# Feed-forward of a two-layer decoder trunk: another placing of the second product's slab jobs, 22 pairs instead of 24 in its right half, later gathers, and four PSUM banks for the last transposes

## The chip, the cores and the metric

The kernel runs on one core of a Trainium2 chip. The metric is the device time of one execution in microseconds, the median over several runs; lower is better. A profile comes from one execution of its own.

## The reference, cut to what matters

Two decoder layers on 256 tokens of width 2048, all in float32. Each layer ends with a squared-ReLU feed-forward of inner width 8192, and that is the part that the change touches:

```python
def squared_relu_mlp(h, w1, w2):
    z = jax.nn.relu(h @ w1)
    return (z * z) @ w2
...
for i in range(DEPTH):                      # DEPTH = 2
    ...                                     # pooling mixer or differential attention
    x = x + jnp.concatenate([token_out, mem_out], axis=-1) @ w_out[i]
    x = x + squared_relu_mlp(rms_norm(x, ffn_norm[i]), w_ff1[i], w_ff2[i])
```

w_ff1 is 2048x8192 and w_ff2 8192x2048, 64 MB each and layer; they are read from DRAM once and used once.

## The kernel before

**Numbers as two halves.** Each float32 operand is split in two: a rounded high part (ACT, a cast, L170) and the remainder (DVE, a subtraction, L173). A product is then high times high, high times low and low times high. For the weights this split runs all through the kernel: SP loads rows of 128x1024 (L139) into four "raw" buffers, ACT and DVE split them into a ring of six slots of 512 columns (hi_ring, lo_ring, and two more called slot), TensorE reads the slots. `Feed` does this in a fixed order: `fill` (L209) prepares up to three jobs ahead of the one that is used, and `load` (L125) issues loads three rows ahead of that.

**Up tiles.** `ffn` (L820) computes the transposed hidden layer in 64 up tiles, "f" 0 to 63. A tile is 16 blocks of 128x128 weights: `narrow` (L906) issues for each block one matmul of the high part with 512 columns (L913) and one of the low part with 256 columns (L915), all into one PSUM bank, x_bank, that `bank` (L973) draws. While slab jobs hold seven banks, one bank of the tag st is left for it. ACT copies the bank out (L927), and after each second tile `convert` (L861) makes of the two tiles a pair: add, ReLU, square, high and low parts into a "spot" of za or zb, and four sums of quarters with their own high and low parts into another spot. There are 16 spots; `left` gives one back when the last reader of its pair is done.

**Slab jobs.** The second product runs while the up tiles still do, by a Strassen scheme with seven products for eight. `slab_jobs` (L976) treats one pair (two blocks of 128 rows of w_ff2) and one half of the output columns, A (the right 1024, called with c + 2) or B (the left 1024), as four jobs, 0 to 3, with 2, 1, 2 and 2 products of three 512-column matmuls each (L1004 to L1006). They accumulate over the pairs of a phase in seven banks, m0 to m2, n0, n1, o and t (`open_banks`, L1013).

The weights of a slab come as two rows. Row a is loaded by SP (L139), and half of row b is then added into it by an accumulating DMA of POOL (L141); row b is loaded by SP. Both use the three buffers of the tag rows: row a of slab n takes the buffer that row b of slab n-2 leaves when the low part of that slab's job 3 has been split off; job 0 needs row a with its sum, job 2 and job 3 need row b after the DVE addition at L204.

**Phases and bank changes.** The banks hold one half of the columns at a time, so PHASES (L285) takes the pairs in five stretches: A 0 to 5, B 0 to 11, A 6 to 17, B 12 to 23, A 18 to 31. Between two of them comes a bank change, `finish_banks` (L1020): ACT copies two banks (L1037, L1038), seven DVE additions (L1039 to L1045) combine the seven products into four corners, and later ticks run the rest, a tick being four blocks of an up tile: `gather` (L1052) adds what an earlier phase of the same half left in DRAM (accumulating POOL DMAs, L1054), `park` (L1056) stores the corners to DRAM (SP, L1058) when the half is not complete, and `scale` (L1067) and `turn` (L1075) scale a complete half, transpose it on TensorE (L1082) and add it to the residual (DVE, L1085).

**What sets the order.** `ffn_plan` (L289) writes the sequence of tiles and jobs. In the gap ahead of each tile it places up to RATE = 4 jobs of the running phase, if the pair is ready; behind the last job of a phase it places the change and no job until the next gap. A pair becomes ready every second tile, so in phase 0 every second gap has four jobs and the others none. From then on a period is one up tile and one slab. B columns of pairs 24 to 31 are left to eight down tiles "d" (`down_tile`, L937), each 16 blocks like an up tile.

Of the kernel before, what the change touches and what calls it, by code (L numbers as in the profile page):

```python
# [18 lines left out]
P = 128  # L19
# [263 lines left out]
STEPS = (1, 2, 3, 4, 6, 7, 8, 10)  # L283
NB = 24
PHASES = (("A", 0, 6), ("B", 0, 12), ("A", 6, 18), ("B", 12, 24), ("A", 18, 32))  # L285
RATE = 4


def ffn_plan(tiles):  # L289

    ready = {}
    for t, what in enumerate(tiles):
        if what[0] == "f" and what[1] % 2:
            ready[what[1] // 2] = t + LAG
# [3 lines left out]
    credit = 0  # L303
    phase = 0
    for t, what in enumerate(tiles):
        credit = min(credit + RATE, 4)
        first = len(items)
        while jobs and credit and ready[jobs[0][1]] <= t and jobs[0][0] == phase:
            items.append(("s", *jobs.pop(0)))
            credit -= 1  # L310
# [39 lines left out]
def program(ctx, tc, plan, dry, xT, memT, par, lam, cst, wst, yT):  # L350
# [469 lines left out]
    def ffn(l, xs, tag, done):  # L820
# [18 lines left out]
        def take():  # L839
            return spare.pop(0)  # L840

# [19 lines left out]
        def convert(i, late):  # L861
# [16 lines left out]
            def high():  # L878
                zat[i] = take()
                due[i] = ["A"] + (["B"] if i < NB else ["N"] * 8)  # L880
                nc.scalar.copy(zs(i)[:, :, 0:T], u)
# [12 lines left out]
            def sums_high():  # L894
                sat[i] = take()
                nc.scalar.copy(sit(i)[:, 0:512].rearrange("p (a c) -> p a c", a=2), sums)
# [40 lines left out]
        def down_tile(q, n, ps):  # L937
            ks = list(range(q * NK, q * NK + NK))
            if l == 1 and q == 3 and n == 7:
                narrow(ps, "w_ff2", n, ks[:12], z)  # L940
# [3 lines left out]
                for k in ks[12:]:  # L944
                    hi, lo = feed.block(("w_ff2", l, k, n, 1))
                    zk = z(k)
                    nc.tensor.matmul(end[:, 0:T], hi, zk[:, 0:T], start=k == ks[12], stop=False)
# [4 lines left out]
                for i in range(24, 32):  # L952
# [7 lines left out]
            for i in range(24, 32):  # L960
# [59 lines left out]
        def finish_banks(p):  # L1020
# [87 lines left out]
        def go(part):  # L1108
            for at_, what in part:
                if what[0] == "s":  # L1110
# [32 lines left out]

        return last, first_down - ups + 4 * 8

# [601 lines left out]
```

## Time and profile before

| what | value |
|---|---|
| device time, median of 3 runs | 2066.78 us (2066.61 to 2066.79) |
| the profiled execution's own time | 2067.66 us |
| its span in the trace | 2065.5 us, 30343 instructions |
| granted TensorE clock over the span | 0.996 |
| DMA | 435.61 MB, 211 GB/s over the span |

The profile is of one execution. Busy times of engines overlap; a busy TensorE is a modelled figure, since matmuls are pipelined. In the timeline a row gives the start in us from the start of the span, the duration, the engine, the line of the kernel, the operation with out<-in, and in square brackets how long the engine had been idle before it and what ended that wait. The feed-forward of the first layer lies at about 252 to 960 us, that of the second at about 1356 to 2060 us.

### The profile page before, as it was taken

Reading aid. Unit: us, or ns where it says so; the run is one execution under the profiler, and the core shown is the slowest. Engines: PE = TensorE matmul, PEld = TensorE weight load, DVE = VectorE, ACT = ScalarE, POOL = GpSimd, SP = SyncE. Lnnn points to the kernel's source line nnn. Section 1 sums busy time; section 2 is a strip of 40 time slices with the busy share of each in tenths; the row PEclk is TensorE's granted clock in tenths of the full one; section 3 lists DMA queues with packets and bytes.
Section 4 is the critical chain, followed back from the end, with each engine's and each line's share of the span. In section 5 each row is a group of like instructions: output and inputs, shape, how many; then the busy total and the mean of one; then the engine's idle time right before and its main releaser. Section 6 shows DMA issues by size and latency. Waiting matters only on the chain.

```text
span 2065.5 us, 30343 instructions
## 1 busy us (share of the span) xinstructions
PE 2016.9 (98%) x10592; PEld 1709.4 (83%) x10592; DVE 1764.8 (85%) x2641; ACT 1368.9 (66%) x2177; POOL 166.2 (8%) x195
## 2 busy tenths in 40 slices
PE   9999999999998999999999999999999999998998
PEld 7888888788886887887888899888878787887887
DVE  8988777999998998988775798877889898898987
ACT  7765566666676666667665697556667676676674
POOL 0002300000001010000000000410000001001000
PEclk9999999999999999999999999999999999999999
DMA  9565656777777786766655645656677778777775
GB/s 312 171 207 187 198 185 207 220 229 235 233 230 229 227 243 201 227 184 205 207 190 190 194 145 177 193 176 205 214 226 230 234 225 236 228 228 214 221 219 159
DMA packets 133642, 435.61 MB, mean 211 GB/s; under 512 B 15152, under 2 KB 18224, under 8 KB 133488
## 3 DMA queue, kind: packets, MB, share of 16 engines
q1 hardware_dynamic: 114912, 398.00, 58.2%
q0 software_dynamic: 18432, 35.66, 10.4%
q8 instruction: 83, 1.36, 0.3%
q14 instruction: 71, 0.58, 0.1%
q10 hardware_dynamic: 144, 0.01, 0.0%
HBM read 422.46 MB, written 8.39 MB: 209 GB/s over the span
## 4 chain that ended last, share of the span: by engine, by line
PE 88%; DMA 6%; DVE 4%; ACT 2%; issue 1%; POOL 0%; SPq 0%; ACTq 0%; POOLq 0%; DVEq 0%
PE x_bank L913 20%; PE x_bank L915 10%; PE p L1006 7%; PE p L1004 7%; PE p L1005 7%; PE wo L504 6%; DMA slab<-in_w 4%; PE wo L506 3%; PE q L535 3%; PE ff L913 3%; PE k L535 3%; PE v L535 3%; PE u L504 2%; PE mk L535 2%; PE mv L535 2%; DVE lo_ring L173 2%
## 5 line engine op out<-in xcount | busy, mean ns | idle before, releaser
L173 DVE TENSOR_TENSOR lo_ring<-raw,hi_ring 128x512 fp32r<-128x512 f32 (+1 forms) x643 | 553.2, 878 | 106.6 <-ACT hi_ring L170 99.2
L170 ACT CAST hi_ring<-raw 128x512 fp32r<-128x512 f32 (+1 forms) x643 | 483.0, 767 | 197.4 <-PE wo L504 61.6
L173 DVE TENSOR_TENSOR lo_ring<-slab,hi_ring 128x1024 fp32r<-128x1024 f32 x336 | 345.5, 1043 | 62.7 <-ACT hi_ring L170 58.1
L170 ACT CAST hi_ring<-slab 128x1024 fp32r<-128x1024 f32 x336 | 304.3, 906 | 115.4 <-DMA slab<-in_w 54.3
L141 POOL DMA_DIRECT2D slab<-in_w x112 | 96.8, 864 | 1648.4 <-ACT hi_ring L170 319.5
L913 PE MATMUL x_bank<-fx,hi_ring 128*128 128x512 f32 x704 | 221.5, 396 | 3.4 <-ACT room L927 3.4
L927 ACT COPY room<-x_bank 128x512 f32<-128x512 f32 x118 | 69.2, 586 | 208.9 <-PE x_bank L915 208.9
L170 ACT CAST slot<-slab 128x1024 fp32r<-128x1024 f32 x112 | 117.4, 1048 | 80.3 <-PE x_bank L913 80.1
L173 DVE TENSOR_TENSOR slot<-slab,slot 128x1024 fp32r<-128x1024 f32 x112 | 136.8, 1222 | 30.0 <-ACT slot L170 30.0
L504 PE MATMUL wo<-cat,hi_ring 128*128 128x512 f32 x512 | 161.6, 396 | 0.0
L915 PEld LDWEIGHTS x_bank<-fx,lo_ring 128*128 128x128 f32 x704 | 132.2, 188 | 31.1
L913 PE MATMUL x_bank<-fx0b,hi_ring 128*128 128x512 f32 x472 | 148.2, 395 | 0.0
L915 PE MATMUL x_bank<-fx,lo_ring 128*128 128x256 f32 x704 | 138.4, 278 | 0.0
L204 DVE TENSOR_TENSOR slab<-slab,slab 128x1024 f32<-128x1024 f32 x112 | 136.5, 1219 | 0.0
L1004 PE MATMUL p<-hi_ring,zb 128*128 128x512 f32 x280 | 112.3, 401 | 7.0 <-ACT hi_ring L170 7.0
L506 PEld LDWEIGHTS wo<-cat,lo_ring 128*128 128x128 f32 x512 | 96.1, 188 | 22.0
L913 PEld LDWEIGHTS x_bank<-fx,hi_ring 128*128 128x128 f32 x704 | 108.9, 189 | 6.4 <-ACT room L927 4.4
L1006 PE MATMUL p<-lo_ring,zb 128*128 128x512 f32 x280 | 109.6, 396 | 3.0 <-DVE lo_ring L173 2.8
L1005 PE MATMUL p<-hi_ring,zb 128*128 128x512 f32 x280 | 110.2, 393 | 0.0
L915 PEld LDWEIGHTS x_bank<-fx0b,lo_ring 128*128 128x128 f32 x472 | 88.7, 188 | 21.0
L506 PE MATMUL wo<-cat,lo_ring 128*128 128x256 f32 x512 | 101.7, 278 | 0.0
L915 PE MATMUL x_bank<-fx0b,lo_ring 128*128 128x256 f32 x472 | 92.7, 278 | 0.0
(525 smaller groups left out, 4679.3 us busy)
## 6 DMA issues: line engine op xcount, KB each, us to landing
raw<-in_w SPq DMA_DIRECT2D x500, 512.0 KB, 4.5
slab<-in_w SPq DMA_DIRECT2D x224, 512.0 KB, 3.5
slab<-in_w POOLq DMA_DIRECT2D x112, 256.0 KB, 4.7
part<-room SPq DMA_DIRECT2D x6, 512.0 KB, 4.4
room<-part POOLq DMA_DIRECT2D x4, 512.0 KB, 7.8
memraw<-in_mem SPq DMA_DIRECT2D x4, 512.0 KB, 3.6
memraw<-in_mem SPq DMA_DIRECT2D x6, 256.0 KB, 6.0
part<-c_x SPq DMA_DIRECT2D x6, 256.0 KB, 4.7
```

The costliest lines, as they stand in the source:

```text
L141: self.nc.gpsimd.dma_start(t[:, 512:1024], self.wst[other, :, 512:1024], accum_op=ALU.add)
L170: cast = self.nc.scalar.copy(hi, src)
L173: self.nc.vector.tensor_sub(lo, src, hi.bitcast(F32))
L204: add(two, t.unsqueeze(1).to_broadcast([P, 2, 512]), two)
L504: nc.tensor.matmul(ps, hi, xs[:, k, :], start=first and j == 0, stop=False)
L506: nc.tensor.matmul(ps[:, T : 2 * T], lo, xs[:, k, 0:T], start=False, stop=last and j == len(ks) - 1,)
L535: nc.tensor.matmul(ps[t], a, b, start=i == 0 and j == 0, stop=i == NK - 1 and j == 2)
L913: nc.tensor.matmul(ps, hi, src(k), start=k == ks[0], stop=False)
L915: nc.tensor.matmul(ps[:, T : 2 * T], lo, src(k)[:, 0:T], start=False, stop=k == ks[-1])
L1004: nc.tensor.matmul(ps, al, hi[:, s], start=i == begin, stop=False)
L1005: nc.tensor.matmul(ps, ah, hi[:, s], start=False, stop=False)
L1006: nc.tensor.matmul(ps, ah, lo[:, s], start=False, stop=i == end - 1)
```

## The change

- NB becomes 22: the B half is done by slab jobs for pairs 0 to 21 only, and the eight down tiles take pairs 22 to 31, 20 blocks each. Their rows are prepared in single jobs of 512 columns (rows_whole off), the up tiles' in whole rows as before.
- RATE and its credit go. A gap of phase 0 takes up to two jobs; the first gap behind a change two, the next three, then four; the last eight tiles two to four by what is left. Since the phases no longer begin with four jobs, job 0 of the next slab now stands in the gap of jobs 1 to 3 of the slab before, and the gap of a change lacks one job.
- The gather of the middle changes comes at tick 10 instead of 5, the park behind it at 15 instead of 9, the first park at 6 instead of 5, the scale of B at 15 instead of 9; the transposes of B begin one gap later and stand behind two jobs. The gather of the last phase stays at 5.
- The four transposes of the last A phase use banks t, o, n0 and n1, one each, instead of t four times.
- There are two more spots. They lie in the memory of the residual's second half (resid.parts[1], 1 MB), which is stored to DRAM at the start of ffn and reloaded behind job 3 of pair 29 in the last phase. `take` gives these two only to pairs and sums that are read out early.

```diff
-NB = 24
-PHASES = (("A", 0, 6), ("B", 0, 12), ("A", 6, 18), ("B", 12, 24), ("A", 18, 32))
-RATE = 4
+NB = 22
+PHASES = (("A", 0, 6), ("B", 0, 12), ("A", 6, 18), ("B", 12, 22), ("A", 18, 32))
...
-        credit = min(credit + RATE, 4)
+        room = 2 if phase == 0 else min(4, 2 + since)
+        if t >= len(tiles) - 8:
+            room = min(4, max(2, len(jobs) - 2 * (len(tiles) - 5 - t)))
+        since += 1
...
-                    turns = {t + 3 + h: h for h in range(4)}
+                    turns = {t + 4 + h: h for h in range(4)}
                 phase += 1
+                since = 0
                 break
...
-            items.insert(first + 1, ("turn", turns[t]))
+            items.insert(first + 2, ("turn", turns[t]))
...
+        kept = dp.tile([P, NK // 2, T], F32, tag="kept", name=f"kept{l}")
+        nc.sync.dma_start(kept, resid.parts[1])
+        more = sp.tile([P, 4, 512], F32R, tag="residb", name=f"more{l}")
+        spots += [more[:, 2 * j : 2 * j + 2, :] for j in range(2)]
...
-            ks = list(range(q * NK, q * NK + NK))
+            ks = list(range(2 * NB, 4 * NK))
...
-                at(5, gather)
+                at(5 if p == len(PHASES) - 1 else 10, gather)
...
-                at(5 if old is None else 9, park)
+                at(6 if old is None else 15, park)
...
-                t4 = bk("t" if half == "A" else "st", "ct", (P, 2, T))
+                t4 = bk(("t", "o", "n0", "n1")[h] if half == "A" else "st", "ct", (P, 2, T))
...
-                at(9, scale)
+                at(15, scale)
...
+                    if (p, i, j) == (4, 29, 3):
+                        assert {16, 17} <= set(spare)
+                        resid.parts[1] = sp.tile(
+                            [P, NK // 2, T], F32, tag="residb", name=f"resid_b{l}"
+                        )
+                        nc.sync.dma_start(resid.parts[1], kept)
...
+                    feed.rows_whole = False
                     down_tile(*what[1:], ps)
```

Three places show how rows move. The first is TensorE in phase 0 of the first layer; x_bank_2930 and x_bank_2978 are the banks of two successive up tiles. Before:

```order
L913 MATMUL x_bank_2930<-fx0b_1740,hi_ring_76 128x512 x2
L915 MATMUL x_bank_2930<-fx0b_1740,lo_ring_77 128x256 x2
L913 MATMUL x_bank_2978<-fx0a_1739,hi_ring_76 128x512 x2
L915 MATMUL x_bank_2978<-fx0a_1739,lo_ring_77 128x256 x2
L913 MATMUL x_bank_2978<-fx0a_1739,hi_ring_76 128x512 x2
```

The same border in the changed kernel, where x_bank_2915 and x_bank_2981 are the two tiles (line numbers are eight higher); p3 to p6 are products of a slab's jobs 2 and 3:

```order
L921 MATMUL x_bank_2915<-fx0b_1740,hi_ring_76 128x512 x2
L923 MATMUL x_bank_2915<-fx0b_1740,lo_ring_77 128x256 x2
L1012 MATMUL p3_2895<-slot0_2625,za0_2622 128x512
L1013 MATMUL p3_2895<-slot0_2625,za0_2622 128x512
L1014 MATMUL p3_2895<-slot0_2625,za0_2622 128x512
...
L1014 MATMUL p6_2898<-lo_ring_77,za0_2622 128x512
L921 MATMUL x_bank_2981<-fx0a_1739,hi_ring_76 128x512 x2
L923 MATMUL x_bank_2981<-fx0a_1739,lo_ring_77 128x256 x2
```

Two jobs, twelve matmuls, now stand between two tiles that were next to each other.

The second place is SP's queue at the third bank change of the first layer, with the corners' stores (part<-c_x, c_y, room), the slab rows (slab) and the up tiles' rows (raw). slab_5514 and slab_5591 are row b of slab 12 and row a of slab 13, slab_5597 and slab_5693 row b of 13 and row a of 14. Before:

```order
L139 DMA slab_5514<-in_w 128x1024
L139 DMA slab_5591<-in_w 128x1024
L139 DMA raw_5709<-in_w 128x1024
L139 DMA raw_5777<-in_w 128x1024
L1058 DMA part_5628<-c_x 128x512
L1058 DMA part_5628<-c_y 128x512
L139 DMA slab_5597<-in_w 128x1024
L139 DMA raw_5795<-in_w 128x1024
L1058 DMA part_5628<-room_2624 128x1024
L139 DMA slab_5693<-in_w 128x1024
```

After, where slab_5798 and slab_5840 are row b of slab 13 and row a of slab 14:

```order
L139 DMA slab_5661<-in_w 128x1024
L139 DMA slab_5750<-in_w 128x1024
L139 DMA raw_5828<-in_w 128x1024
L139 DMA raw_5838<-in_w 128x1024
L1066 DMA part_5772<-c_x 128x512
L1066 DMA part_5772<-c_y 128x512
L139 DMA raw_5903<-in_w 128x1024
L139 DMA raw_5922<-in_w 128x1024
L1066 DMA part_5772<-room_2624 128x1024
L139 DMA slab_5798<-in_w 128x1024
L139 DMA slab_5840<-in_w 128x1024
```

Row b of slab 13 moves behind the last store; the stores keep their place between row a of 13 and row a of 14.

The third place is DVE in a steady period. slab_5954 is row b of a slab, slab_6031 row a of the next, lo_ring<-slab a split. Before:

```order
L204 TENSOR_TENSOR slab_5954<-slab_5948,slab_5954 128x1024
L885 TENSOR_TENSOR zb_2623<-room_2624,zb_2623 128x2x256
L889 TENSOR_TENSOR room_2624<-room_2624 128x256
L892 TENSOR_TENSOR room_2624<-room_2624 128x128
L173 TENSOR_TENSOR lo_ring<-slab_5954,hi_ring 128x1024
L173 TENSOR_TENSOR slot_2625<-raw_6047,slot_2625 128x1024
L900 TENSOR_TENSOR zb_2623<-room_2624,zb_2623 128x512
L173 TENSOR_TENSOR lo_ring<-raw_6112,hi_ring 128x1024
L173 TENSOR_TENSOR lo_ring<-slab_6031,hi_ring 128x1024
L201 TENSOR_TENSOR slab_6031<-slab_6031 128x512
```

After, with slab_6065 and slab_6148 as rows b and slab_6096 as row a of the next slab:

```order
L204 TENSOR_TENSOR slab_6065<-slab_6010,slab_6065 128x1024
L173 TENSOR_TENSOR lo_ring<-slab_6065,hi_ring 128x1024
L173 TENSOR_TENSOR lo_ring<-slab_6096,hi_ring 128x1024
L878 TENSOR_TENSOR room_2624<-room_2624 128x2x256
L201 TENSOR_TENSOR slab_6096<-slab_6096 128x512
L173 TENSOR_TENSOR lo_ring<-raw_6158,hi_ring 128x1024
L173 TENSOR_TENSOR slot_2625<-raw_6177,slot_2625 128x1024
L173 TENSOR_TENSOR lo_ring<-slab_6096,hi_ring 128x512
L173 TENSOR_TENSOR lo_ring<-slab_6148,hi_ring 128x1024
L893 TENSOR_TENSOR za_2622<-room_2624,za_2622 128x2x256
L204 TENSOR_TENSOR slab_6148<-slab_6096,slab_6148 128x1024
```

The split of row a's job 0 now follows that of job 3 directly, and the two raw rows come between job 0 and job 3 of one slab instead of ahead of job 0.

More of the change, by code (lines that the diff above doesn't have):

```diff
@@ L302, in ffn_plan @@
     turns = {}
-    credit = 0
-    phase = 0
+    phase = since = 0
     for t, what in enumerate(tiles):
-        credit = min(credit + RATE, 4)
+        room = 2 if phase == 0 else min(4, 2 + since)
+        if t >= len(tiles) - 8:
+            room = min(4, max(2, len(jobs) - 2 * (len(tiles) - 5 - t)))
+        since += 1
         first = len(items)
-        while jobs and credit and ready[jobs[0][1]] <= t and jobs[0][0] == phase:
+        while jobs and room and ready[jobs[0][1]] <= t and jobs[0][0] == phase:
             items.append(("s", *jobs.pop(0)))
-            credit -= 1
+            room -= 1
             if not jobs or jobs[0][0] != phase:
@@ L878, in high @@
             def high():
-                zat[i] = take()
+                zat[i] = take(i >= NB)
                 due[i] = ["A"] + (["B"] if i < NB else ["N"] * 8)
@@ L894, in sums_high @@
             def sums_high():
-                sat[i] = take()
+                sat[i] = take(i > 28)
                 nc.scalar.copy(sit(i)[:, 0:512].rearrange("p (a c) -> p a c", a=2), sums)
@@ L937, in down_tile @@
         def down_tile(q, n, ps):
[L938 removed]
+            ks = list(range(2 * NB, 4 * NK))
             if l == 1 and q == 3 and n == 7:
[L940 removed]
+                narrow(ps, "w_ff2", n, ks[:-4], z)
                 end = mmt("end")
@@ L943, in down_tile @@
                 add_down(n, douts[downs[0] % 2])
-                for k in ks[12:]:
+                for k in ks[-4:]:
                     hi, lo = feed.block(("w_ff2", l, k, n, 1))
                     zk = z(k)
-                    nc.tensor.matmul(end[:, 0:T], hi, zk[:, 0:T], start=k == ks[12], stop=False)
+                    nc.tensor.matmul(end[:, 0:T], hi, zk[:, 0:T], start=k == ks[-4], stop=False)
                     nc.tensor.matmul(end[:, 0:T], hi, zk[:, T : 2 * T], start=False, stop=False)
@@ L951, in down_tile @@
                 tick()
-                for i in range(24, 32):
+                for i in range(NB, 32):
                     left(i, "N")
@@ L959, in down_tile @@
             narrow(ps, "w_ff2", n, ks, z)
-            for i in range(24, 32):
+            for i in range(NB, 32):
                 left(i, "N")
@@ L1142, in last @@
             feed.rows_whole = False
-        return last, first_down - ups + 4 * 8
+        return last, first_down - ups + 4 * (32 - NB)
     big = sp.tile([P, 4096], F32, tag="big", name="big0")
```

6 lines of the change are left out of this document (4 added, 2 removed).

## The prediction

> **What bounds the kernel now.** I read the page first, for the share of each engine, then the timeline of TensorE for the price of a tile and a slab, then the table of windows, to set each stretch of the feed-forward against its content, and last the waits and the chain of waits where a stretch came out too long.
>
> ```profile
> span 2065.5 us, 30343 instructions
> PE 2016.9 (98%) x10592; PEld 1709.4 (83%) x10592; DVE 1764.8 (85%) x2641; ACT 1368.9 (66%) x2177; POOL 166.2 (8%) x195
> 663.01 0.62 PE L913 MATMUL x_bank<-fx0a,hi_ring 128*128 128x512 f32 x2
> 668.59 0.40 PE L1004 MATMUL p<-slot,zb 128*128 128x512 f32 x1
> ```
>
> TensorE is the bound; DVE, at 85%, is next. An up tile runs from 663.01 to 668.59, 5.58 us, so a block of sixteen is 0.349. Columns of the windows: stretch, length, busy time and instructions of PE, PEld, DVE, ACT and POOL, granted clock, DMA share, GB/s.
>
> ```profile
> 290.79:375.05 84.26, 80.88 (x426) 68.71 (x425) 68.83 (x85) 53.87 (x72) 4.30 (x5) 1.00 0.66 206
> 375.05:419.19 44.14, 42.62 (x214) 34.72 (x213) 40.87 (x49) 29.34 (x37) 3.43 (x4) 1.00 0.77 234
> 419.19:501.96 82.77, 82.77 (x426) 70.44 (x424) 77.02 (x92) 57.46 (x73) 6.90 (x8) 1.00 0.78 231
> 501.96:545.99 44.03, 42.56 (x213) 34.79 (x212) 40.94 (x49) 29.37 (x37) 3.45 (x4) 1.00 0.77 238
> 628.76:678.70 49.94, 44.09 (x214) 34.41 (x212) 40.94 (x49) 28.92 (x37) 4.98 (x6) 1.00 0.80 231
> 761.47:831.92 70.45, 67.16 (x335) 55.10 (x334) 62.55 (x75) 46.16 (x59) 6.47 (x8) 0.98 0.73 216
> 893.92:959.65 65.73, 59.65 (x317) 50.99 (x316) 54.18 (x85) 43.90 (x71) 1.72 (x2) 0.95 0.56 173
> 1394.74:1479.01 84.27, 80.89 (x426) 68.72 (x425) 68.84 (x85) 53.88 (x72) 4.30 (x5) 1.00 0.67 203
> 1479.01:1524.32 45.31, 43.11 (x213) 34.62 (x212) 40.85 (x49) 29.32 (x37) 3.43 (x4) 1.00 0.76 231
> 1606.99:1653.12 46.13, 43.41 (x214) 34.55 (x212) 40.87 (x49) 29.34 (x37) 3.45 (x4) 1.00 0.73 223
> 1735.94:1784.85 48.91, 44.88 (x213) 35.75 (x212) 40.94 (x49) 28.93 (x37) 4.98 (x6) 0.97 0.83 237
> 1867.64:1939.12 71.48, 66.14 (x336) 53.66 (x335) 62.55 (x75) 46.31 (x59) 7.06 (x9) 1.00 0.76 215
> 2001.22:2059.80 58.58, 55.94 (x312) 48.06 (x311) 45.44 (x64) 31.07 (x41) 1.72 (x2) 1.00 0.57 174
> ```
>
> The third row is a steady stretch: eight periods of one up tile and one slab without a wait, 82.77 / 8 = 10.35 each, so a slab is 10.35 - 5.58 = 4.77 and one of its seven products 0.68. Every other row is set against that.
>
> - Phase 0 (rows 1 and 8): ten tiles and five slabs are 79.65; lost 4.61 and 4.62, together 9.2.
> - Bank changes: four periods are 41.38, so rows 2, 4 and 5 lose 2.76, 2.65 and 8.56, rows 9 to 11 lose 3.93, 4.75 and 7.53. Rows 6 and 12 hold six periods (62.08) and four transposes at 0.45 (1.8): 6.57 and 7.60. Together 44.35.
> - Tails (rows 7 and 13): eight down tiles (44.64), two slabs (9.54) and four transposes are 55.98; the second ends four blocks earlier, 54.59. Lost 9.75 and 3.99, together 13.74.
>
> In all 67.3 us of 2067.66 are no work, and the change turns on these.
>
> ```profile
> PE p L1004 <- ACT hi_ring L170: 12.0, 15, 2.5
> PE x_bank L913 <- ACT room L927: 8.1, 12, 0.7
> PE p L1006 <- DVE lo_ring L173: 6.3, 13, 0.6
> PE ct L1082 <- DVE residb L1085: 5.5, 2, 4.2
> 291.85 0.73 PE L913 MATMUL x_bank<-fx0a,hi_ring 128*128 128x512 f32 x2 [0.68 <-ACT room L927]
> 948.11 0.47 PE L1082 MATMUL ct<-const,c_a 128*128 128x128 f32 x1 [4.17 <-DVE residb L1085]
> 954.07 0.27 PE L1082 MATMUL ct<-const,c_b 128*128 128x128 f32 x1
> 954.28 0.27 PE L1082 MATMUL ct<-const,c_b 128*128 128x128 f32 x1
> ```
>
> The last two start 0.21 apart with one between them: about 0.11 per transpose, 0.45 for the four of a turn.
>
> **The change, part by part.**
>
> *Two jobs a gap in phase 0.* The waits on the eviction (L927) come where two up tiles share the one bank back to back; a lost 4.61 over five such borders is 0.92 each. Two jobs, 12 matmuls or about 2 us, now stand at every border, more than 0.92. Saved 9.2.
>
> *The ramp 2, 3, 4 and the missing job behind a change.* One up tile more stands ahead of the jobs that need the first copied bank, and DVE's seven additions and the splits queued behind them get 5.58 us more. Changes 0-1 and 1-2 lose 2.65 to 4.75 now; 5.58 more covers that, but the additions still sit ahead of the splits on a DVE that is 93% busy in steady gaps (77.02 of 82.77). I leave 1.0 each, ends 0 and 2.65.
>
> *The later gather, third change.*
>
> ```profile
> 622.69 0.68 DVE L1039 TENSOR_TENSOR c_y<-c_x,p 128x512 f32<-128x512 f32 x1
> 637.48 0.33 SPq L1058
> 637.90 7.98 DMA slab<-in_w
> 646.43 6.62 DMA slab<-in_w
> 653.20 1.06 ACT hi_ring L170
> 654.28 1.23 DVE lo_ring L173
> ```
>
> The additions begin at 622.69, the change's end. The store of the gathered corners (L1058) cannot go before the gather has landed, at end + 14.8, and row a of slab 14 is queued behind it on SP: it is loaded in 7.98, summed in 6.62 and ready at 653.05, end + 30.4. The changed order keeps that sequence. Job 0 of slab 14 is wanted after three tiles and fourteen products, 3 x 5.58 + 14 x 0.68 = end + 26.3; with cast and split ahead of it the stall is 4 to 6. The later tick moves the gather in the written order only: on POOL it follows the sum for slab 13 in both, so I let it land no later (if the tick, four blocks or 1.4 us, were a time, five of them would add 7). Jobs 2 and 3 of slab 13 need their row at end + 23.5 instead of 17.9. So 4.5 remains of 8.56 and 7.53, ends 1 and 11. At the fourth change, where nothing is parked, 1.5 remains of 6.57 and 7.60, ends 0 and 6.57. Per layer the changes keep 1 + 1 + 4.5 + 1.5 = 8, both layers 16.
>
> A wait of 4.5 us in one piece has a second price: behind the 4.17 us wait at 948.11 the transposes took 0.47 us where the later ones took 0.27. At half speed for at most the 5.9 us up to the rows at 954, that is up to 2.5 a layer. My sum leaves it out, since waits on splits were 2.5 us at the longest.
> The Trainium skill (TensorE: Matmul & The Clock Gate, section "Why this matters for your kernels") asks for no idle gaps of over some 3 us, since one window of idle halves the clock; the trace agrees with it at 948.11, and by it the time would be some 5 us above mine, 2038.
>
> *22 pairs instead of 24.* A layer gains 8 tiles x 4 blocks = 32 blocks x 0.349 = 11.16 and loses two slabs, 9.54: +1.6, both layers +3.2.
>
> *Turns of B* stand behind two jobs and share the bank st with x_bank; I put 1 a layer, ends 0 and 2: 2.
>
> *Steady periods.* A slab's chain runs through two periods, 20.70.
>
> ```profile
> slab<-in_w SPq DMA_DIRECT2D x92, 512.0 KB, 4.0
> slab<-in_w POOLq DMA_DIRECT2D x46, 256.0 KB, 4.6
> 570.43 2.35 DVE L173 TENSOR_TENSOR lo_ring<-raw,hi_ring 128x1024 fp32r<-128x1024 f32 x2
> ```
>
> Freed buffer, load 4.0, issue 0.55 (from 645.88 to 646.43), sum 4.6, cast 1.06: 10.2. Then DVE must go from job 0's split to job 3's, which frees the buffer again. Two raw splits and a conversion, about 3.0 (2.35 and 0.68), stood outside this stretch and now stand in it, so that it is a whole period of DVE's work, 77.02 / 8 = 9.63. The loop grows from 16.8 to 19.8 of 20.70; 0.9 is left. Landings vary, and I take a quarter of the 42 loops (21 a layer) as 0.57 too long: 6. Ends: 0, and 42 by how far the mean exceeds 10.0, which rival c prices.
> The Trainium skill (DMA: Bandwidth & Descriptors, section "Anatomy of one DMA — SWDGE (gpsimd) path") gives 2.0 us plus the bytes at 436 GB/s, by estimate 2.6 for POOL's 256 KB; by that nothing would drift and the time were 2027. The trace has 4.6, and the measurement decides.
>
> *The kept half of the residual.* Its store waits for the last residual addition and blocks SP until then.
>
> ```profile
> 252.93 0.42 DVE L811 TENSOR_TENSOR residb<-residb,wo 128x256 f32<-128x256 f32 x1
> 256.12 0.33 SPq L139 DMA_DIRECT2D raw<-in_w  x1
> 263.24 1.05 ACT L170 CAST hi_ring<-raw 128x1024 fp32r<-128x1024 f32 x1 [1.74 <-PE ff L913]
> ```
>
> The addition ends at 253.35 and SP's next load was issued at 256.12, so nothing is held; a cast waits for TensorE at 263.24, so the 1 MB beside it costs 0. The reload in the last phase goes into SP's queue between slab rows, with 1 MB where a row has 0.5: 2 x 4.0 = 8 us of queue at most, mostly under the slack; 1.5 a layer, ends 0 and 4: 3.
>
> *Tails.* The two single-bank waits go (a job in every gap up to d4), and the four turns have a bank each: the 4.17 and the half speed behind it go. 1.7 and 1.2 remain: 2.9.
>
> The sum: remaining 0 + 16 + 2.9 of 67.3, new 3.2 + 2 + 6 + 3 = 14.2; 67.3 - 18.9 - 14.2 = 34.2 saved, 2067.66 - 34.2 = 2033.5 for a profiled execution. That execution lies 0.88 over the median of the runs shown (2066.78), so the median becomes 2033.
>
> **The rivals.** (a) *All slack holds.* The steady loop never runs over, the reload is hidden and the changes keep about 0.6 each: 2.9 + 5 + 2 + 3.2 = 13.1 remain in place of 33.1, 2013. For it: steady TensorE has no wait at all today. Against: the 7.98 and 6.62 landings behind a park.
>
> (b) *The handover persists.* The store still holds SP behind a gather that is now later, and changes 2-3 and 3-4 cost what they cost: 8.56 + 7.53 + 6.57 + 7.60 = 30.3 instead of 12, 2051. For it: the rows of SP keep their order around the stores. Against: row b of slab 13 is wanted 5.6 us later.
>
> (c) *Slower: the slab chain becomes the bound.* Place: every steady period; price: 42 loops by the excess of load, issue, sum and their issue gaps over 10.0. The saving without drift is 40.2, so it decides at an excess of 0.96, a mean of 11.0; at 11.5 the loss is 62, and the time 2089. For it: 7.98 + 0.55 + 6.62 = 15.2 occurred. Against: medians of 4.0 and 4.6 make 9.2, and three rows are loaded ahead.
>
> (d) *It does little:* the waits move from the changes to the gaps with four jobs and the drift takes the rest: within 4 us of 2066.
>
> **How the numbers follow.** Forecast 0.58, a 0.13, b 0.17, c 0.08, d 0.04. 0.2%, about 4 us, is what a measurement of this kernel can tell from no change. The range goes from a to somewhat above b, 2012 to 2055; c and d lie outside, 0.12. Faster by more than 0.2% are the forecast, a and b: 0.88; same 0.04; slower 0.08.
>
> **What would show it.** In the profile after: waits of x_bank on the eviction gone from phase 0; windows of phase 0 at their content; the slab jobs' wait on the cast (12.0 us at L1004) shrunk, the largest left behind the third change; steady periods at 10.35 plus at most 0.3; no 4 us wait ahead of a transpose. I am wrong if steady periods grow by over 0.5 (c), or if windows behind the third and fourth change are as long as before (b).

## The result: slower by 1.3%, and the profile after

The changed kernel takes 2095.39 us (median of four runs, 2090.73 to 2100.72) against 2066.78 for the one before: the ratio is 1.0133, 95% interval 1.0102 to 1.0164. The forecast was 2033 us, and its rival (c), with a chance of 0.08, is what happened: the sign that the prediction gave for it, steady periods longer by over 0.5, is there. The profiled execution took 2100.72 us, 33.1 more than that of before.

From the page of the changed kernel, the span and the busy times:

```profile
span 2098.9 us, 30696 instructions
PE 2037.2 (97%) x10636; PEld 1700.5 (81%) x10636; DVE 1758.5 (84%) x2665; ACT 1359.2 (65%) x2209; POOL 163.5 (8%) x191
```

The windows of the changed kernel, with the columns as in the prediction: phase 0 of the first layer (ten tiles, five slabs), eight steady periods of the first and of the second layer, the down tiles at the end of the second layer, and the stretch between the two feed-forwards.

```profile
280.22:359.78 79.56, 79.56 (x427) 68.34 (x426) 68.93 (x86) 55.76 (x72) 4.34 (x5) 1.00 0.70 216
403.49:494.20 90.71, 85.68 (x426) 69.40 (x425) 76.48 (x88) 55.92 (x73) 6.91 (x8) 1.00 0.71 208
1526.93:1618.79 91.86, 86.19 (x426) 69.38 (x424) 76.84 (x88) 56.13 (x73) 6.92 (x8) 1.00 0.70 206
2061.42:2088.47 27.05, 27.05 (x157) 23.60 (x155) 19.33 (x36) 16.17 (x29) 1.73 (x2) 1.00 0.59 169
973.84:1374.76 400.92, 397.91 (x2156) 341.66 (x2154) 317.33 (x724) 276.70 (x643) 27.29 (x31) 1.00 0.59 188
```

Phase 0 is at its content (79.65 by the prediction's prices): the 9.2 us are gained. The steady stretch, which was the reference without a wait at 82.77, is now 90.71 and 91.86: 17.0 us more over 16 slabs, 1.06 each. The planner makes 40 such gaps a layer, with jobs 1 to 3 of one slab and job 0 of the next. The 72 of both layers that can be cut out whole, without a transpose in them, hold 829.1 us, where the prices of before (10.35 each, 11.75 beside a down tile of 20 blocks) make 756.4: 73 us, 1.0 each. The waits of TensorE lie at the same places:

```profile
PE p L1014 <- DVE lo_ring L173: 18.1, 41, 0.5
PE x_bank L923 <- DVE lo_ring L173: 14.7, 23, 0.7
PE p L1012 <- ACT hi_ring L170: 9.5, 21, 1.2
PE ct L1090 <- ACT room L935: 4.0, 2, 2.8
```

The four lines of before held 2 to 15 waits each, of up to 4.2 us. Now there are many short ones, 41 and 23 times at most 0.7 us, on the low halves that DVE makes, and they come in every phase behind phase 0. They are not the whole loss: in the windows above the busy time of TensorE, which is modelled, has grown too (85.68 and 86.19 for 82.77).

Where they come from is read in the chain of waits of one steady period (start, duration, what):

```profile
417.40 4.10 DMA slab<-in_w
421.56 0.49 issue
422.05 6.39 DMA slab<-in_w
428.59 1.06 ACT hi_ring L170
429.68 1.23 DVE lo_ring L173
431.42 0.69 DVE slab L201
432.11 1.15 DVE lo_ring L173
433.30 0.50 PE x_bank L923 x2
```

Three rows of ACT and DVE from the timeline of the same period:

```profile
428.59 1.05 ACT L170 CAST hi_ring<-slab 128x1024 fp32r<-128x1024 f32 x1 [2.36 <-DMA slab<-in_w]
429.68 1.23 DVE L173 TENSOR_TENSOR lo_ring<-slab,hi_ring 128x1024 fp32r<-128x1024 f32 x1 [2.19 <-ACT hi_ring L170]
439.03 1.23 DVE L173 TENSOR_TENSOR lo_ring<-slab,hi_ring 128x1024 fp32r<-128x1024 f32 x1 [0.18 <-ACT hi_ring L170]
```

A row's load of 4.10, its sum of 6.39, the cast at the very moment the sum lands, job 0's split; ACT has stood idle for 2.36 and DVE for 2.19 before them. DVE then catches up, and the raw split behind (432.11) is what TensorE waits for at 433.30. Job 3's split ends at 439.03 + 1.23 = 440.26 and frees the buffer for the next load: the loop takes 440.26 - 417.40 = 22.9 us where two periods are 20.70. Nothing is late by much in any one place; the loop is longer than the time it has.

Two things made it longer. DVE needs 10.6 us from the start of job 0's split to the end of job 3's, and the landings grew. The DMA issues of the changed kernel between 400 and 900 us (KB each, median us to landing), which were 4.0 and 4.6 before:

```profile
slab<-in_w SPq DMA_DIRECT2D x84, 512.0 KB, 4.3
slab<-in_w POOLq DMA_DIRECT2D x42, 256.0 KB, 6.1
```

The reason for the slower sum shows in the timeline, in the issue times of SP's raw rows around a sum of POOL. In the kernel before:

```profile
570.54 0.33 SPq L139 DMA_DIRECT2D slab<-in_w  x1
571.68 1.47 SPq L139 DMA_DIRECT2D raw<-in_w  x2
574.46 0.86 POOL L141 DMA_DIRECT2D slab<-in_w  x1 [8.80 <-DVE room L888]
```

In the changed kernel:

```profile
443.37 2.06 SPq L139 DMA_DIRECT2D raw<-in_w  x2
444.97 0.86 POOL L141 DMA_DIRECT2D slab<-in_w  x1 [11.65 <-DMA slab<-in_w]
```

Before, both raw loads had gone out by 573.15, 1.3 us ahead of the sum at 574.46. After, the pair takes until 445.43, past the sum's issue at 444.97, so that the second lies beside it: a raw load waits for the split that frees its buffer, and the raw splits now follow job 0's. These are two sums; the experiments below ask whether it holds in general.

### The profile page after: what moved, and what is told of

The parts are those of the page before. It is cut to its first block, busy times and chain, and to the rows that moved or that the text cites. A ratio compares the mean times of both kernels' runs of the same rounds, so it can differ in the third digit from the quotient of the medians.

```text
span 2098.9 us, 30696 instructions
## 1 busy us (share of the span) xinstructions
PE 2037.2 (97%) x10636; PEld 1700.5 (81%) x10636; DVE 1758.5 (84%) x2665; ACT 1359.2 (65%) x2209; POOL 163.5 (8%) x191
## 4 chain that ended last, share of the span: by engine, by line
PE 65%; DVE 13%; DMA 13%; ACT 4%; issue 4%; DVEq 0%; SPq 0%; ACTq 0%; POOLq 0%
PE x_bank L921 13%; DMA slab<-in_w 12%; DVE lo_ring L173 7%; PE x_bank L923 7%; PE wo L506 6%; PE p L1014 4%; PE p L1012 4%; PE p L1013 4%; ACT hi_ring L170 3%; PE wo L508 3%; PE q L537 3%; PE k L537 3%; PE v L537 3%; PE ff L921 3%; PE u L506 2%
## 5 line engine op out<-in xcount | busy, mean ns | idle before, releaser
L173 DVE TENSOR_TENSOR lo_ring<-raw,hi_ring 128x512 fp32r<-128x512 f32 (+1 forms) x695 | 584.1, 854 | 125.7 <-ACT hi_ring L170 118.9
L170 ACT CAST hi_ring<-slab 128x1024 fp32r<-128x1024 f32 (+1 forms) x312 | 291.2, 941 | 288.4 <-DVE slab L204 198.4
L173 DVE TENSOR_TENSOR lo_ring<-slab,hi_ring 128x1024 fp32r<-128x1024 f32 (+1 forms) x312 | 336.1, 1088 | 122.7 <-ACT hi_ring L170 121.4
L170 ACT CAST slot<-slab 128x1024 fp32r<-128x1024 f32 (+1 forms) x120 | 113.0, 941 | 94.2 <-DVE slab L204 77.6
L173 DVE TENSOR_TENSOR slot<-slab,slot 128x1024 fp32r<-128x1024 f32 (+1 forms) x120 | 130.6, 1088 | 36.5 <-ACT slot L170 34.8
L921 PE MATMUL x_bank<-fx0a,hi_ring 128*128 128x512 f32 x440 | 138.2, 395 | 1.2 <-DVE resida L1093 1.2
L923 PEld LDWEIGHTS x_bank<-fx0a,lo_ring 128*128 128x128 f32 x440 | 81.2, 188 | 33.2 <-DVE lo_ring L173 15.4
L921 PE MATMUL x_bank<-fx0b,hi_ring 128*128 128x512 f32 x312 | 98.0, 395 | 0.0
L923 PE MATMUL x_bank<-fx0a,lo_ring 128*128 128x256 f32 x440 | 88.4, 282 | 8.4 <-DVE lo_ring L173 8.4
L1012 PE MATMUL p<-hi_ring,zb 128*128 128x512 f32 x217 | 87.9, 405 | 4.3 <-ACT hi_ring L170 4.1
L1013 PE MATMUL p<-hi_ring,zb 128*128 128x512 f32 x217 | 85.4, 394 | 0.0
```

The costliest lines, as they stand in the source:

```text
L170: cast = self.nc.scalar.copy(hi, src)
L173: self.nc.vector.tensor_sub(lo, src, hi.bitcast(F32))
L921: nc.tensor.matmul(ps, hi, src(k), start=k == ks[0], stop=False)
L923: nc.tensor.matmul(ps[:, T : 2 * T], lo, src(k)[:, 0:T], start=False, stop=k == ks[-1])
L1012: nc.tensor.matmul(ps, al, hi[:, s], start=i == begin, stop=False)
L1013: nc.tensor.matmul(ps, ah, hi[:, s], start=False, stop=False)
```

## The experiments

Theory A: the loop of the three slab row buffers bounds the steady periods, since job 0 of one slab and job 3 of the slab before now share a gap and their splits follow each other. Rival B: the time went to something else that is new (20-block down tiles, the two spots, the kept half, 22 pairs). Rival D: a DVE that is nearly full bounds it in its new order, whatever the buffers.

### The same change, with whole slabs in a gap again

```diff
-        room = 2 if phase == 0 else min(4, 2 + since)
+        room = 2 if phase == 0 or since < 2 else 4
```

> The changed kernel with one line other: a gap takes two jobs in the first two gaps behind a change and four from then on, so that each later gap again holds jobs 0 to 3 of one slab; the number of jobs per change that come later is the same. Theory A (the loop of the slab's row buffers runs past two periods because job 0 and job 3 of neighbouring slabs now stand in one gap): steady periods back to 10.35 us, and 2020 to 2035 us. Rival B (the time went to what else is new: 20-block down tiles, two spots more, the kept half of the residual, 22 pairs): the periods stay long and the time 2085 or more.

Measured: 2028.24 us (2027.63 to 2031.48), 0.9813 of the kernel before (0.9794 to 0.9832; before 2067.99 on this chip). One line turns the change from 1.3% slower into 1.9% faster. Eight steady periods of this variant:

```profile
412.51:495.34 82.83, 82.83 (x425) 70.42 (x424) 76.09 (x89) 56.93 (x72) 6.90 (x8) 1.00 0.78 229
```

DVE does the same work as in the slow kernel (76.09 against 76.48 us), in 82.83 instead of 90.71. Everything that B names is still there, so B falls as the cause of the loss.

### The shift alone, in the kernel before

```diff
-        credit = min(credit + RATE, 4)
+        credit = min(4, 2 + since) if phase == 2 else RATE
+        since += 1
```

> The kernel before with the new ramp (2, 3, 4) behind the second bank change only, so that the 12 slabs of the third phase, in both layers, have job 0 in the gap of the slab before; everything else as before. Theory A: about 0.94 us more per slab, as measured in the changed kernel's second phase, 11 slabs and two layers, some +21, against at most 5 to 7 saved at the two changes: 2076 to 2090 us, slower than before. Rival B (it takes the 20-block down tiles, the extra spots or the kept half): the ramp alone saves 3 to 8 us.

Measured: 2077.45 us, 1.0061 of the kernel before (1.0045 to 1.0076). This is the cleanest comparison of the study, since one execution holds both orders: eight periods of the second phase, whole slabs, and eight of the third, shifted.

```profile
419.33:501.99 82.66, 82.66 (x425) 70.41 (x424) 77.03 (x92) 57.44 (x73) 6.90 (x8) 1.00 0.77 232
531.71:622.06 90.35, 85.95 (x426) 69.48 (x424) 76.92 (x91) 56.73 (x73) 6.90 (x8) 1.00 0.71 211
```

7.7 us more for the same eight tiles and eight slabs, without any other part of the change. The sums of the two stretches, in the same order:

```profile
slab<-in_w POOLq DMA_DIRECT2D x8, 256.0 KB, 4.6
slab<-in_w POOLq DMA_DIRECT2D x8, 256.0 KB, 6.5
```

### Four slab rows, and its control

```diff
-SLOTS, AHEAD, LOADS, KOFF, RAWS = 6, 3, 3, 2, 4
+SLOTS, AHEAD, LOADS, KOFF, RAWS = 6, 3, 3, 2, 3
...
-                t = self.rows.tile([P, 1024], F32, tag="rows", bufs=3, name=f"slab{h}")
+                t = self.rows.tile([P, 1024], F32, tag="rows", bufs=4, name=f"slab{h}")
...
```

The other tiles of the tag rows get four buffers too.

> The changed kernel with four slab row buffers instead of three; for the memory, three raw buffers instead of four. Theory A: row a of a slab no longer waits for the split of job 3 two slabs before, the casts of job 0 no longer start at the landing of the sum, and the time is 2020 to 2040 us, unless the three raw buffers starve the up tiles. Rival D (the new order of the splits on a DVE that is nearly full is what PE waits for, whatever the buffers): 2085 or more, with DVE's waits as they are.

The control has the first edit only:

> The changed kernel with three raw buffers instead of four and nothing else: the control for the four slab rows. Theory A has nothing to say beyond that it stays slow: 2090 to 2110 us. If it becomes much faster, raw rows issued later make room for the slab sums, and contention between them is the cause.

Measured: 2038.24 us with the fourth row (0.9856, 0.9834 to 0.9878) and 2098.39 without (1.0147, 1.0124 to 1.0170). Eight steady periods of the two, the one with four rows first:

```profile
406.74:491.06 84.32, 83.53 (x426) 70.03 (x425) 76.46 (x88) 55.95 (x73) 6.89 (x8) 1.00 0.75 225
```

```profile
407.21:495.90 88.69, 85.03 (x425) 69.67 (x424) 76.27 (x88) 56.66 (x73) 6.89 (x8) 1.00 0.73 213
```

With the job order and DVE's order of the slow kernel and one buffer more, 60 us go. D falls: it is the buffer that is waited for.

### Without the sum

```diff
-            if r[0] == "S" and r[2] == 0:
+            if False:
                 self.nc.gpsimd.dma_start(
```

> The changed kernel without the accumulating DMA that adds half of row b into row a of each slab (that addition is left out, everything else is done). Theory A: the loop loses issue, landing and cast delay of that DMA, some 6.5 of 22.5 us, and falls under 20.7: steady periods at 10.35, 2010 to 2030 us. Rivals B and D: the periods stay long, 2080 or more.

Measured: 2017.50 us (0.976, 0.9739 to 0.9781). The eight periods are at their content, with the job order of the slow kernel:

```profile
403.65:486.31 82.66, 82.66 (x425) 70.43 (x424) 76.41 (x88) 56.31 (x72) 0.00 (x0) 1.00 0.64 204
```

### Half the bytes in the raw rows

The raw rows are loaded 512 columns wide, and cast and split read these twice.

```diff
+            if r[0] == "N" and n == 1024:
+                n = 512
...
+        if job[0] == "R":
+            half, a2 = src[:, 0:512], lambda x: x.rearrange("p (a c) -> p a c", a=2)
+            src, hi2, lo2 = half.unsqueeze(1).to_broadcast([P, 2, 512]), a2(hi), a2(lo)
...
-            if not self._split(p, self.raw[r][:, c : c + 512], 1):
+            if not self._split(p, self.raw[r][:, 0:512], 1):
```

> The changed kernel with raw rows of 128x512 instead of 128x1024, their 512 columns used twice by cast and split (half of these weights are left out; engines do the same work, the raw rows bring half the bytes). It asks why the slab's sum landed in 6.1 us in the changed kernel and in 4.6 before. Theory C (contention: in the changed order the raw loads are issued beside the sum): the sum lands in 4.6 or less, the loop of 22.5 us loses 1.5 to 2.5 and the steady loss mostly goes: 2030 to 2050 us. Theory O (the longer stretch on DVE between the splits of job 0 and job 3 is enough by itself): 2075 or more.

Measured: 2029.32 us (0.981, 0.9791 to 0.9829), a touch under the range. Landings and eight periods of this kernel:

```profile
slab<-in_w SPq DMA_DIRECT2D x89, 512.0 KB, 3.3
slab<-in_w POOLq DMA_DIRECT2D x44, 256.0 KB, 5.0
```

```profile
403.31:488.63 85.32, 83.97 (x426) 69.86 (x424) 76.46 (x88) 55.94 (x73) 6.90 (x8) 1.00 0.61 172
```

The slab's row and sum land 1.0 and 1.1 us earlier, and two thirds of the steady loss go (90.71 to 85.32). What else is in flight thus bears on the loop. How much of the loss the new order of the loads made is not shown by this: the row lands in 3.3 us here, which is less than the 4.0 of before, while the sum, still beside a raw load, did not reach the expected 4.6.

### The order of the splits alone

TensorE's order is left as changed; in the list of preparations job 0 is put behind the two raw rows that follow it. On DVE a raw split then stands between job 3's and job 0's split in about every second period.

```diff
+        for i in range(1, len(prep) - 2):
+            three = prep[i - 1][0] == "S" and prep[i - 1][2] == 3
+            if three and prep[i][0] == "S" and prep[i][2] == 0:
+                if prep[i + 1][0] == "R" and prep[i + 2][0] == "R":
+                    prep[i : i + 3] = prep[i + 1], prep[i + 2], prep[i]
```

> The changed kernel with TensorE's order as it is, but with job 0's preparation asked for behind the two raw rows that follow it instead of ahead of them, so that in about every second period a raw split stands between job 3 and job 0 as before. If the order of the splits makes the loop long (a longer stretch from job 0's cast to job 3's split, and raw loads beside the sum), the steady loss falls by a third to a half with it: 2055 to 2080 us. If the place of job 0 on TensorE is what counts (its slots are used late), it stays: 2088 to 2102.

Measured: 2064.25 us (0.9984, 0.9971 to 0.9997), 31 less than the changed kernel's 2095.39, with half of the steady loss:

```profile
404.36:491.21 86.85, 85.87 (x425) 70.27 (x424) 77.56 (x89) 57.40 (x72) 6.89 (x8) 1.00 0.75 218
```

With TensorE's order unchanged, the order of the preparations alone is worth half of the steady loss, so the place of job 0 on TensorE is not what that half hangs on. A full undoing was not tried, so that the other half is not told apart.

### Parts of the change by themselves

Two jobs a gap in phase 0, in the kernel before:

```diff
-        credit = min(credit + RATE, 4)
+        credit = 2 if phase == 0 else RATE
```

> The kernel before with two slab jobs a gap in phase 0 and nothing else. The prediction's term: the 9.2 us lost to the single bank in the two first stretches go, nothing else moves: 2057 to 2061 us against 2068 for the kernel before on this chip. Rival: the jobs' splits now run two by two and DVE or the slab rows hold phase 0 back: less than 4 us gained.

Measured: 2063.91 us (0.999, 0.9979 to 1.0002): not told from no change, and outside the expectation. The waits of the up tiles on the copy of their bank (L927) did go, as the waits of TensorE in this kernel show, but another line grew:

```profile
PE p L1004 <- ACT hi_ring L170: 19.4, 18, 3.5
PE x_bank L913 <- ACT room L964: 1.4, 2, 0.7
```

The slab jobs' waits on the cast were 12.0 before (17.0 with those on the casts into slot, L1004, which are gone) and are 19.4 now. In the first layer what phase 0 gains is given back behind it: with both feed-forwards begun within 0.3 us, the next part of the program starts at 959.15 instead of 959.74. In the second layer some 5 us stay in the profiled execution. The rival had the size, but for another reason; phase 0 itself runs without a wait. Why the later phases of the first layer cost more was not tried.

The old ticks for gather, park and scale, in the aligned variant:

```diff
-                at(5 if p == len(PHASES) - 1 else 10, gather)
+                at(5, gather)
...
-                at(6 if old is None else 15, park)
+                at(5 if old is None else 9, park)
...
-                at(15, scale)
+                at(9, scale)
```

> The aligned variant (two jobs in the first two gaps behind a change, then four) with the old places of gather, park and scale (5, 5 and 9, 9). The prediction's reading that on POOL and SP the order of the stores between the slab rows is what counts and the later tick is worth little: within 4 us of the aligned variant, 2025 to 2033. Rival: the later places are what shortens the changes: 2036 to 2050.

Measured: 2028.84 us (0.9823, 0.9803 to 0.9843). The later ticks are worth nothing that can be told.

One bank for the four last transposes, in the aligned variant:

```diff
-                t4 = bk(("t", "o", "n0", "n1")[h] if half == "A" else "st", "ct", (P, 2, T))
+                t4 = bk("t" if half == "A" else "st", "ct", (P, 2, T))
```

> The aligned variant with the four last transposes of each layer in bank t as before, not in four banks. The prediction's term: the 4.17 us wait, the half clock behind it and 1.3 us in the second layer come back, 5 to 9 us, 2033 to 2038. Rival: the waits came from somewhere else in the order of the last tiles (four blocks more per tile now) and the bank is worth under 2 us.

Measured: 2039.76 us (0.9877, 0.9855 to 0.9898), 11.5 over the aligned variant and more than expected. The down tile in which these transposes lie, in the first layer: the wait in the timeline with one bank, the window of the tile with one, and then with four banks:

```profile
929.69 0.47 PE L1090 MATMUL ct<-const,c_a 128*128 128x128 f32 x1 [5.67 <-DVE resid_b L1093]
```

```profile
920.39:935.22 14.83, 9.16 (x45) 8.04 (x44) 10.05 (x22) 11.74 (x25) 0.00 (x0) 0.77 0.62 224
```

```profile
920.64:927.82 7.18, 7.16 (x46) 6.19 (x45) 3.54 (x8) 6.03 (x13) 0.00 (x0) 1.00 0.54 196
```

7.65 us in this tile alone, with a wait of 5.67 and a mean clock of 0.77.

The stores of the third change from POOL's queue instead of SP's, in the aligned variant:

```diff
-                    nc.sync.dma_start(part[half][:, c, :], side)
+                    (nc.sync if old is None else nc.gpsimd).dma_start(part[half][:, c, :], side)
```

> The aligned variant with the stores behind the third change issued by POOL instead of SP, so that SP's slab rows no longer stand behind the gather. The prediction's reading of the third change (the store holds SP until the gather lands): its loss, 4.1 and 3.6 us in the aligned variant, falls to about 1 each, 2021 to 2025 us against 2028. Rival: POOL's own queue, which now holds the next slab's sum behind the gather and the stores, keeps the loss where it is: 2027 to 2032.

Measured: 2025.08 us (0.9801, 0.9782 to 0.9821), five runs from 2024.15 to 2029.48, so that the gain of 3.2 over the aligned variant is near what can be told. The period behind the third change (10.35 without a wait), the aligned variant first, then this one, in both layers:

```profile
652.40:666.88 14.48, 12.55 (x55) 9.68 (x53) 11.64 (x15) 9.81 (x13) 0.86 (x1) 0.88 0.75 253
1739.68:1753.65 13.97, 11.50 (x55) 8.56 (x53) 11.84 (x15) 9.37 (x12) 0.86 (x1) 1.00 0.78 267
```

```profile
652.85:664.55 11.70, 10.90 (x54) 8.73 (x53) 11.45 (x15) 8.54 (x12) 1.12 (x2) 1.00 0.89 292
1734.65:1747.59 12.94, 11.32 (x54) 8.57 (x53) 10.43 (x13) 9.25 (x12) 1.28 (x2) 1.00 0.82 279
```

4.1 and 3.6 us become 1.4 and 2.6, where about 1 each was expected: the store on SP was part of that stall, about half.

Four rows and three raw buffers in the aligned variant (both edits of above):

> The aligned variant with four slab row buffers and three raw buffers. If the row buffers still cost the aligned variant its last losses (7.8 and 14.8 us in the two layers), 2012 to 2022 us; if the three raw buffers cost more than that, 2028 to 2040.

Measured: 2034.15 us (0.9838, 0.9821 to 0.9855), 5.9 over the aligned variant: taken together the two edits cost. That it is the raw buffer that is given up is not shown, for the aligned variant was not run with that edit alone.

The reloads of the memory tokens in the slab rows' buffers, on top of the stores on POOL:

```diff
-        mraw[p] = wp.tile([P, 4, T], F32, tag="raw", bufs=RAWS, name="memraw1")
+        mraw[p] = tp.tile([P, 4, T], F32, tag="rows", bufs=3, name="memraw1")
```

> The variant with the stores on POOL, with the two reloads of the memory tokens behind the first feed-forward in the slab rows' buffers instead of the raw rows'. It asks where the 4.5 us between the layers come from that the changed kernel has more than the one before. Theory: SP holds the next raw rows behind such a reload that waits for a raw buffer; then the wait of mk on its cast goes and the time falls by 1 to 4: 2021 to 2024. Rival: the wait comes from the raw rows' order itself: 2025 as without it.

Measured: 2023.27 us (0.9789, 0.9775 to 0.9803), the fastest kernel of this study that does the whole work. The stretch between the feed-forwards was 396.34 before and is 400.92 in the changed kernel; here it is in the aligned variant and in this one:

```profile
933.86:1336.33 402.47, 398.89 (x2155) 342.81 (x2154) 316.83 (x725) 276.67 (x645) 27.28 (x31) 1.00 0.58 187
```

```profile
931.75:1328.81 397.06, 397.06 (x2155) 341.88 (x2154) 315.85 (x723) 275.74 (x643) 27.25 (x31) 1.00 0.58 187
```

Of these 5.4 us the edit can claim little. The kernel with the stores on POOL, whose reloads still take raw buffers, has 397.98 in its profile, so 4.5 are gone without it. Against that kernel the waits of mk on its cast fall from 2.0 to 0.3 us, as expected, and the median by 1.8, but the runs of the two overlap (up to 2024.43 here, from 2024.15 there).

## Why the prediction failed, step by step

**Bound and prices.** Right: tiles, slabs and products kept their prices, and the content of every stretch came out as worked out (phase 0: 79.56 against 79.65).

**Phase 0, 9.2 us.** Right where it stands. (Twelve matmuls are four products, 2.7 us by the prediction's own price and not about 2; that was on the safe side.) That the gain may be handed back later, as in the first layer of the kernel before with only this edit, was not considered.

**Ramp and changes, 16 us left.** Right in kind. In the aligned variant, the third change kept 4.1 and 3.6 us where the forecast had 4.5, about half of it for the reason given, the store on SP behind the gather; what makes the other half is open. That the later ticks would not matter there was right as well.

**Tails, 2.9 us left.** Right: the last tiles of the second layer run without a wait (27.05 of 27.05), and the four banks are worth 11.5 us in the aligned variant. That this is near what the forecast had for the tails as a whole (13.7 - 2.9 = 10.8) is partly luck, for the forecast counted the waits on the one bank of the up tiles in it too, and the four banks alone were expected to bring 5 to 9.

**Turns of B, 2 us.** Under-sized: 4.0 us in two waits, one of 2.80 with half speed behind it, on the eviction of the one bank st.

**Steady periods, 6 us.** This step failed, by a factor of some 12: it cost 73 in the 72 periods counted above. The mechanism was named, the place and the direction were right, and the point from which it decides was too. What failed is the size of its terms: "Landings vary, and I take a quarter of the 42 loops (21 a layer) as 0.57 too long: 6." The loop was put at 19.8 us with the landings of before, 4.0 and 4.6, although the same paragraph moved the raw splits, and with them the raw loads, to the place beside the sum. In the chain shown the sum took 6.39 instead of 4.6, load, issue and cast 0.3 more, and DVE from job 0 to job 3 10.6 instead of 9.63: together 3.0, 22.86 for 19.84. So a loop, two periods, ran over by 2.2 us in this chain and by 2.0 in the mean of the 72 periods, where the forecast let a quarter run over by 0.57. By rival (c)'s formula the quantity that was put at 9.2 is 11.0 in this chain (4.10 + 0.49 + 6.39), with 10.0 as the start and 11.0 as break-even; with DVE's 1.0 more on top it is beyond that. Rival (c) gave 2089 for an excess of 1.5 (42 x 1.5 is 63 and not 62, which changes nothing); the median came out at 2095. With 73 for 6 the forecast's own sum gives 2100.5 for a profiled execution, and it took 2100.72. So close a fit is luck, since other terms were off both ways.

The range of 2012 to 2055 left rival (c) outside, on the argument "medians of 4.0 and 4.6 make 9.2". Those medians belong to an order that the change dissolved.

The Trainium skill (DMA: Bandwidth & Descriptors, section "Anatomy of one DMA — SWDGE (gpsimd) path") has a formula by which the sum would take an estimated 2.6 us. It is further off: the median was 4.6 in the kernel before and 6.1 in the changed one. The forecast did not rest on it.

**Reload and kept half, 3 us.** The reload lies in the steady stretches and could not be told apart. Not forecast at all were 4.6 us more between the feed-forwards in the profiled execution. In the last experiment another buffer for the reload of the memory tokens brought 1.8, in another variant; where the rest comes from is open.

**What stays open:** how the 3.0 us of the loop divide between contention and DVE's order in the mean over all periods (halving the raw bytes took two thirds, moving half of the splits took half, and the two act on each other), and why two jobs a gap in phase 0 alone make what follows in the first layer dearer.

## What to carry to other kernels

A stretch that runs without a wait has a slack, and the first question to a new order is how much of it is left in each buffer's loop: from the moment a buffer is freed, through load, cast and use, to the moment it is freed again, set against the periods it has. Work that loop out with the landings that the new order will have, not with those of the old: if it moves loads beside each other, the landing of before is the lower end. When a plan shifts work by a fraction of its period, try the variant that shifts by whole units first; here one line in the planner was worth 67 us.

## What the runs showed of the hardware

**An accumulating DMA feels its neighbours.** The same 256 KB sum landed in a median of 4.6 us with the raw loads issued ahead of it, 6.1 with one or two issued beside it, and 5.0 with those of half the bytes. In one execution of the kernel with the shift in one phase both occur, 4.6 and 6.5.

**The length of a wait does not decide by itself on half speed.** In the changed kernel a wait of 2.80 us was followed by a granted clock of 0.57 over four us, and in the aligned variant a wait of only 1.86 stood ahead of a half-speed stretch. Half speed is a granted clock of 0.50. The wait in the timeline and the window behind it, of the changed kernel and then of the aligned variant:

```profile
823.07 0.33 PE L1090 MATMUL ct<-const,c_x 128*128 128x128 f32 x1 [2.80 <-ACT room L935]
```

```profile
823.00:827.00 4.00, 3.93 (x13) 3.22 (x14) 4.00 (x6) 3.48 (x6) 0.86 (x1) 0.57 0.25 43
```

```profile
656.05 0.71 PE L1012 MATMUL p<-hi_ring,zb 128*128 128x512 f32 x1 [1.86 <-ACT hi_ring L170]
```

```profile
657.00:659.00 2.00, 2.00 (x6) 1.61 (x6) 1.97 (x4) 2.00 (x4) 0.79 (x1) 0.50 0.22 28
```

A wait of 2.29 us at 998.49 in the changed kernel was followed by 1.00. The prediction left this price out for waits under 2.5 us. The Trainium skill (TensorE: Matmul & The Clock Gate, section "Why this matters for your kernels") puts it at gaps of over some 3 us. The traces bear that out for every longer wait (3.14, 4.00, 5.67), but those from 1.9 to 2.8 sometimes brought half speed too.

What tells the two kinds apart is where the wait lies. In the kernel before, half speed begins at 789.88, 946.89 and 1752.43, which are whole multiples of 3.413 us apart, and lasts 3.41 or 6.83, but for the end of the program. In the changed kernel, cut into stretches of 3.41 counted from its half speed at 823.32, the first row ends where half speed begins, and the other two share the wait of 2.29 between them:

```profile
819.91:823.32 3.41, 0.61 (x4) 0.25 (x3) 0.76 (x1) 1.83 (x3) 0.00 (x0) 1.00 0.62 220
993.98:997.40 3.42, 2.22 (x10) 1.50 (x8) 2.37 (x6) 1.66 (x5) 0.00 (x0) 1.00 0.96 341
997.40:1000.81 3.41, 2.32 (x9) 1.63 (x10) 2.34 (x5) 2.99 (x7) 0.00 (x0) 1.00 0.07 26
```

TensorE is idle for 2.80 us in the first and for 1.20 and 1.09 in the others. Cut so, away from the two ends of the program and where the clock was full, every stretch of these traces with 1.86 us idle or more was followed by half speed and none with under 1.7; between these both occur.

**A later tick need not move a DMA.** In the aligned variant the first DMA of the third change's gather went out at 634.34 us with the gather at tick 10, and at 634.24 with it at tick 5; the time (2028.24 and 2028.84) and the period behind that change in the first layer (14.48 and 14.94) did not tell the two apart.
